# Diagonal products of two scan chunks in one run, for a one-core hybrid SSD and attention layer

## The chip, the cores and the metric

The kernel runs on one core of one Trainium2 chip. The metric is the device time of one execution in microseconds (us). The engines are named as in the profile: PE is TensorE (the matrix unit), PEld its weight loads, DVE is VectorE, ACT is ScalarE, POOL is GpSimd, SP is the engine that issues most DMA transfers. Every engine works through its own queue in order. They wait for one another through semaphores. PSUM is the memory that PE writes to, in banks of 128 partitions by 512 fp32 numbers.

## The reference

One layer of a diffusion backbone over 512 latent tokens of width 1024, with 256 context tokens beside them. A projection feeds two mixers, a bidirectional state-space scan (SSD) and windowed attention. Their outputs are gated, merged and projected, and a gated convolutional FFN follows. The part that matters here is the scan. It has 32 heads in four groups of eight; a head has 64 channels and the state 128 entries. The tokens are worked in chunks of 128, so four latent chunks per group:

```python
cb = jnp.einsum('bclgn,bcsgn->bgcls', cc, bc)
scores = cb[:, :, None] * jnp.exp(segsum(ac))
y_diag = jnp.einsum('bgrcls,bcsgrp->bclgrp', scores, xc)
y_off = jnp.einsum('bclgn,bcgrpn,bgrcl->bclgrp', cc, states[:, :-1], jnp.exp(cs))
```

`y_diag` is the **diagonal product**: a chunk's 128 by 128 matrix of scores and decays for each head, times the chunk's inputs. `y_off` is the far part, which comes from the states of earlier (and, for the backward scan, later) chunks. Afterwards a skip term `d_skip * xs` is added, and the sum is multiplied with the gate `silu(z)`; the row sums of its squares go into an RMS norm before the output projection of the branch. All of it is fp32.

## The kernel before, in words

Most of PE's work is large projections. Each fp32 operand is split into a high and a low part, and three matmuls replace one (`gemm`, lines 238, 239 and 241). The weights come by DMA and are split on the way: ACT casts the high part (line 183) and DVE subtracts it (line 184). The scan of group g is woven into the projections for group g+1, and in the last group into projections of the gates `z` and `g`. The scan's small steps are put between the steps of a `gemm` through the list `BETWEEN`, of which `gemm` takes one entry at every third step.

For one chunk c of a group the scan does this:

- `chunk_in(c)` loads the decays (`fb`), makes the score matrix `cb` on PE (line 1696), and takes its diagonal (`cbd`, line 1698) for the skip coefficient `coef`. For c > 0 POOL makes a diagonal matrix `dg` (line 1709) that carries the skip. ACT builds two tiles `E` of four heads each and, in two PSUM banks `eb`, the other direction's decays (lines 1719 and 1722). DVE merges them (line 1723), ACT takes the exponential (line 1726), and DVE multiplies with `cb` (line 1730). For c > 0 POOL adds `dg` (line 1732).
- `chunk_out(c)` is a **cluster** of fp32 matmuls on PE: the far products of both directions (line 1754, 16 passes), then the diagonal products of the eight heads into the bank `yd` (line 1762, 16 passes), then the new forward state (`advance`, line 1597, not for c = 3). The diagonal products have only 64 channels each, so PE works them in its 128 by 64 shape, two heads side by side. The other matmuls use the full 128 by 128 shape. DVE scales the far parts by the decays into `te` (line 1756), and POOL adds the two into `y` (line 1770).
- `late()` runs some steps of a projection later. For c = 0 only, where there is no `dg`, PE adds the skip to `yd` by transposing a tile `dx` into it (line 1778). DVE adds `yd` to `y` (line 1779). POOL multiplies with the gate into `zs` (line 1785), or DVE does for c = 3 (line 1783). Squares of the group before are summed by ACT and POOL (`square`, lines 1570 and 1571): in `late` of chunks 0 and 3 and in `chunk_in` of chunks 2 and 3, for all groups but the first.

After the fourth chunk `gate()` stores the four gated tiles of the group (`yz_d`, line 1798). After the last group the kernel loads these tiles back (line 1840), splits them (lines 1842 and 1843) and starts the branch's output projection.

The order on each engine is made by a planner that simulates the program and takes, on each engine, the ready instruction that stands earliest in the program. A few instructions are pinned behind the one before them on their engine (`keep_in_program_order`). POOL's operations of the scan are all pinned (`gp`, `gs`), so POOL goes through them strictly as they are written. PSUM banks called `mis` (five of them) serve `cb`, `eb`, the far products, `yd`, the state products and the transposes. The buffers in question: `E` has three buffers, `y` one (tag `tf`), the gate tiles two (tag `zs`), and the tag `th` one buffer that `dx` and the squares `sq` share.

Of the kernel before, what the change touches and what calls it, by code (L numbers as in the profile page):

```python
# [9 lines left out]
F32 = mybir.dt.float32  # L10
# [3 lines left out]
ALU = mybir.AluOpType  # L14
# [4 lines left out]
P = 128  # L19
# [25 lines left out]
def tile_hybrid_layer(  # L45
# [32 lines left out]
    V, S, G, T = nc.vector, nc.scalar, nc.gpsimd, nc.tensor  # L78
# [3 lines left out]
    hpool = ctx.enter_context(tc.tile_pool(name="hpool", bufs=1))  # L82
# [13 lines left out]
    def bank(name):  # L96
        pool, w = banks_[name]
        return pool.tile([P, 512 * w], F32, tag=name, name=name)
# [11 lines left out]
    def misb():  # L110
        return bank("mis")
# [3 lines left out]
    def tmp(tag):  # L115
        return tpool.tile([P, 512], F32, tag=tag, name=tag, bufs=TMP[tag])
# [27 lines left out]
    for j, t in enumerate((wdn[0], DSUMS[1], DSUMS[2], DSUMS[5], DSUMS[4], wdn[1], wdn[3])):  # L144
        for u in range(DU):
            n = min(2, DK - 2 * u) * HC
# [99 lines left out]
    ident = cpool.tile([P, P], F32, name="ident")  # L246
# [181 lines left out]
    with tc.tile_pool(name="spool", bufs=1) as sp:  # L428
# [237 lines left out]
        for j in range(KT):  # L666
# [46 lines left out]
            x = ("hi", "lo") if j >= NU else ("hh", "hl")  # L713
# [31 lines left out]
        for n in range(2):  # L745
            for j in range(KT):
                x = ("hi", "lo") if j >= NU else ("hh", "hl")
# [668 lines left out]
    zp = zpool.enter_context(tc.tile_pool(name="zpool", bufs=1, side="right", reuse_waits="tile"))  # L1416
    bp = bpool.enter_context(tc.tile_pool(name="bpool", bufs=1, reuse_waits="tile"))
# [15 lines left out]
    def flat(a):  # L1433
        return a.rearrange("p a b -> p (a b)")

    def h8(a):
        return a.rearrange("p (h d) -> p h d", h=8)

    def bc64(a):
        return a.unsqueeze(2).to_broadcast([P, 8, 64])  # L1440
# [132 lines left out]
    def gp(*a):  # L1573
        return tc.keep_in_program_order(G.tensor_tensor(*a))
# [4 lines left out]
    def ssd_steps(g):  # L1579
        d = GR[g]  # L1580
# [10 lines left out]
        def weigh_in(dr, c, place="xw"):  # L1591
            return weigh(d["xs"], c, TD[:, c, dr, 8 * g : 8 * g + 8], place)

        def advance(s, dr, c, xw):
            z0 = 32 * dr + 8 * g
            ps = misb()
            T.matmul(ps, d["Bk"][:, c, :], xw, start=True, stop=True)  # L1597
            n = new_state(dr)
            gp(h8(n), h8(s), bc64(eT[:, z0 : z0 + 8, c]), ALU.mult)
            V.tensor_tensor(n, n, ps, ALU.add)  # L1600
            return n
# [63 lines left out]
        def far_in(c, g=g):  # L1665

            far = bp.tile([P, 2, 4, P], F32, tag="far", name="far", bufs=2)
            for u in range(2):
                a = bass.AP(
                    tensor=us_d.tensor, offset=us_d[c, u, 0, g].offset, ap=[[0, 64], [16 * P, 2], [1, 512]]  # L1670
                )
                dma = nc.sync.dma_start(far[64 * u : 64 * u + 64].rearrange("p r j t -> p r (j t)"), a)
                if not g and not c:
                    tc.add_manual_dep(dma.ins, M_LOADS["x", 16].ins.name, QUEUED, reason="decays behind a projection's weights")
            GR[g]["far", c] = far

        def chunk_in(c):
# [4 lines left out]
            for dr in range(2):  # L1682
                f = bp.tile([P, 8, P], F32, tag="fb", name="fb", bufs=4)
                a = bass.AP(
                    tensor=cs_d.tensor, offset=cs_d.offset + (32 * dr + 8 * g) * L + c * P, ap=[[0, P], [L, 8], [1, P]]
                )
# [3 lines left out]
                fb.append(f)  # L1690
            d["E"] = []

# [18 lines left out]

            def decays():
                for q in range(2):
                    E = bp.tile([P, 4, P], F32, tag="E", name="E", bufs=3)
                    eb = misb()
                    F4 = fb[0][:, 4 * q : 4 * q + 4, :]
                    for u in range(4):
                        h = 8 * g + 4 * q + u
                        e0 = S.activation(E[:, u, :], F4[:, u, :], AF.Identity, bias=TX[:, c, 0, h : h + 1])
                        if u == 0 and c:  # L1720
                            tc.keep_in_program_order(e0)
                        S.activation(eb[:, u * P : (u + 1) * P], fb[1][:, 4 * q + u, :], AF.Identity, bias=TX[:, c, 1, h : h + 1])
                    V.copy_predicated(E, sel.unsqueeze(1).to_broadcast([P, 4, P]), eb.rearrange("p (h l) -> p h l", h=4))
                    d["E"].append(E)
                for E in d["E"]:
                    S.activation(flat(E), flat(E), AF.Exp)

# [18 lines left out]
        def chunk_out(c):  # L1746
            xs, E, far = d["xs"], d["E"], d.pop(("far", c))
            tok = slice(c * P, (c + 1) * P)
            parts = []
            for dr, s in ((0, d["Sf"]), (1, d["Sb"][c])):  # L1750
                ps = misb()
                for ct in range(4):
                    z = slice(ct * P, (ct + 1) * P)
                    T.matmul(ps[:, z], s[:, z], d["CT"][:, tok], start=True, stop=True)  # L1754
                t = tmp("te")
                V.tensor_tensor(t, ps, flat(far[:, dr]), ALU.mult)
                parts.append(t)

            yd = misb()
            for h in range(8):  # L1760
                o = yd[64 * (h % 2) : 64 * (h % 2) + 64, (h // 2) * P : (h // 2 + 1) * P]
                T.matmul(o, xs[:, c, h * 64 : (h + 1) * 64], E[h // 4][:, h % 4, :], start=h < 2, stop=c > 0 and h > 5)
            dx = None
            if not c:
                dx = zp.tile([P, 512], F32, tag="th", name="dx", bufs=1)
                gp(h8(dx), h8(xs[:, c, :]), bc64(d["coef"]), ALU.mult)
            if c < 3:
                d["Sf"] = advance(d["Sf"], 0, c, weigh_in(0, c))
            y = bp.tile([P, 512], F32, tag="tf", name="y", bufs=1)
            gp(y, parts[0], parts[1], ALU.add)  # L1770

            def late():

                if c < 3:
                    far_in(c + 1)
                for ct in range(0 if c else 4):
                    z = slice(ct * P, (ct + 1) * P)
                    tc.keep_in_program_order(T.matmul(yd[:, z], dx[:, z], ident, start=False, stop=ct == 3, is_transpose=True))
                tc.keep_in_program_order(V.tensor_tensor(y, yd, y, ALU.add))
                z = d["zt"][:, :, tok]  # L1780
                x = y.rearrange("p (a t) -> p a t", a=4)
                if c == 3:
                    V.tensor_tensor(z, x, z, ALU.mult)
                else:
                    gp(z, x, z, ALU.mult)
                if g and c in (0, 3):
                    square()

            assert not BETWEEN
            if g < 3:  # L1790
                BETWEEN.extend([lambda: None] * 4 + [lambda: (late(), turn(1)), turn])
            else:
                BETWEEN.extend([lambda: None] * 2 + [late])
# [116 lines left out]
    q2 = hpool.tile([P, L], F32, name="q2")  # L1910
# [535 lines left out]
```

## Time and profile before

| what | value |
|---|---|
| median of three runs | 1214.91 us (1214.61 to 1216.62) |
| the profiled execution | 1215.35 us, of which its span 1213.6 us |
| busy PE, DVE, ACT, POOL | 99%, 76%, 56%, 22% of the span |
| granted PE clock | 0.999 of full speed |
| the stretch with the scans | about 430 to 716 us |

The profile shows one execution. The span runs from the first to the last instruction, and 1.75 us of the profiled execution's time lie outside it. Busy PE says little by itself here, because overlapping matmuls count as busy; what counts is how far apart two neighbours start. In rows of the timeline the columns are start, duration, engine, line, operation, tiles and count, with idle time and its releaser in brackets. In rows of the chain of waits they are start, length, engine, tile, line and count.

### The profile page before, as it was taken

The page shows a single profiled execution, that of the slowest core. Times are in us where ns is not written, and L with a number is a line of the kernel's source. Part 1 is how long each engine was busy: PE and PEld are TensorE (multiplying, and loading weights), DVE is VectorE, ACT ScalarE, POOL GpSimd, SP SyncE. Part 2 cuts the span into 40 slices and gives each one's busy share as a digit, 9 for nine tenths or more (in the row PEclk, how much of TensorE's full clock was granted, in tenths as well). Part 3 has the DMA queues.
Part 4 walks back from the last instruction along what each step waited for, and adds up shares of the span by engine and source line. Part 5 has one row for each costly group of instructions (what it writes and reads, how often), then busy time and mean ns, then how long its engine had stood idle before and what let it go on. Part 6 is the DMA issues. An engine that isn't in the chain of part 4 may idle for free.

```text
span 1213.6 us, 17847 instructions
## 1 busy us (share of the span) xinstructions
PE 1203.6 (99%) x6429; PEld 1005.6 (83%) x6429; DVE 918.6 (76%) x1476; ACT 684.4 (56%) x1269; POOL 263.8 (22%) x274
## 2 busy tenths in 40 slices
PE   9999999999999999999999999999999999999998
PEld 6798888888878878788787887888988888888886
DVE  4857887888565588788887978677677767668787
ACT  4557887778543467476575664223544343436654
POOL 0000121100102546264382762000200100110021
PEclk9999999999999999999999999999999999999999
DMA  9655889844747737566477668687266634437662
GB/s 367 253 148 185 161 229 271 170 133 139 170 140 240 228 113 199 157 162 192 145 178 264 176 228 265 221 251 242 50 163 148 195 117 138 130 107 226 213 185 97
DMA packets 129417, 224.30 MB, mean 185 GB/s; under 512 B 27336, under 2 KB 70640, under 8 KB 129328
## 3 DMA queue, kind: packets, MB, share of 16 engines
q1 hardware_dynamic: 115248, 195.61, 52.0%
q0 software_dynamic: 13792, 27.27, 10.1%
q8 instruction: 51, 0.84, 0.3%
q14 instruction: 38, 0.31, 0.1%
q10 hardware_dynamic: 288, 0.27, 0.1%
HBM read 196.17 MB, written 45.02 MB: 199 GB/s over the span
## 4 chain that ended last, share of the span: by engine, by line
PE 90%; DMA 3%; DVE 2%; POOL 2%; issue 1%; ACT 1%; SPq 0%; DVEq 0%; POOLq 0%; ACTq 0%
PE acc L241 18%; PE acc L238 18%; PE acc L239 18%; PE score L979 3%; PE po L1028 3%; PE pt L1015 2%; PE mis L582 2%; PE mis L1754 2%; PE mis L1597 2%; PE mis L2304 2%; PE mis L2302 2%; PE mis L2303 2%; DMA xs_d<-xb 1%; PE acc L2304 1%; PE acc L2302 1%
## 5 line engine op out<-in xcount | busy, mean ns | idle before, releaser
L184 DVE TENSOR_TENSOR wlo<-wraw,whi 128x1024 fp32r<-128x1024 f32 (+1 forms) x115 | 148.3, 1289 | 89.2 <-ACT whi L183 88.3
L183 ACT CAST whi<-wraw 128x1024 fp32r<-128x1024 f32 (+1 forms) x115 | 120.2, 1046 | 154.2 <-PE acc L239 103.4
L238 PE MATMUL acc<-hlh,whi 128*128 128x512 f32 x472 | 192.8, 409 | 0.0
L241 PE MATMUL acc<-hlh,wlo 128*128 128x512 f32 x472 | 185.6, 393 | 0.0
L239 PE MATMUL acc<-hll,whi 128*128 128x512 f32 x472 | 185.0, 392 | 0.0
L238 PE MATMUL acc<-mh,whi 128*128 128x512 f32 x368 | 143.3, 389 | 0.0
L239 PE MATMUL acc<-ml,whi 128*128 128x512 f32 x368 | 143.2, 389 | 0.0
L241 PE MATMUL acc<-mh,wlo 128*128 128x512 f32 x368 | 143.2, 389 | 0.0
L241 PEld LDWEIGHTS acc<-hlh,wlo 128*128 128x128 f32 x472 | 88.6, 188 | 19.9 <-issue 0.5
L238 PEld LDWEIGHTS acc<-hlh,whi 128*128 128x128 f32 x472 | 88.8, 188 | 17.6 <-issue 2.8
L239 PEld LDWEIGHTS acc<-hll,whi 128*128 128x128 f32 x472 | 88.9, 188 | 17.4 <-issue 2.2
L238 PEld LDWEIGHTS acc<-mh,whi 128*128 128x128 f32 x368 | 69.1, 188 | 14.4
L241 PEld LDWEIGHTS acc<-mh,wlo 128*128 128x128 f32 x368 | 69.1, 188 | 14.3
L239 PEld LDWEIGHTS acc<-ml,whi 128*128 128x128 f32 x368 | 69.1, 188 | 14.2
L164 POOL DMA_DIRECT2D dsum<-wdn x24 | 25.3, 1118 | 194.3 <-DVE wlo L1112 183.7
L988 DVE CUSTOM_DVE_ANT_0 p<-score,winm,nsink 128x512 f32<-128x512 f32 (+1 forms) x64 | 51.8, 810 | 15.3 <-PE score L979 13.8
L995 ACT ACTIVATE p<-p,mneg 128x512 f32<-128x512 f32 (+1 forms) x64 | 49.7, 777 | 15.4 <-DVE mneg L988 14.9
L813 DVE SCALAR_TENSOR_TENSOR tm<-wraw,csil,tm 128x512 f32<-128x512 f32 x56 | 45.9, 819 | 13.1 <-DMA wraw<-wm 12.4
L1023 DVE TENSOR_TENSOR ptl<-pt,pth 128x512 fp32r<-128x512 f32 x72 | 47.5, 685 | 8.4 <-ACT pth L1019 7.7
L238 PE MATMUL acc<-hch,whi 128*128 128x256 f32 x176 | 53.2, 302 | 0.0
L1112 DVE TENSOR_TENSOR wlo<-wraw,whi 128x1024 fp32r<-128x1024 f32 x30 | 36.7, 1223 | 18.3 <-ACT whi L1109 18.2
L241 PE MATMUL acc<-hch,wlo 128*128 128x256 f32 x176 | 49.8, 283 | 0.0
(458 smaller groups left out, 3054.3 us busy)
## 6 DMA issues: line engine op xcount, KB each, us to landing
wraw<-wup SPq DMA_DIRECT2D x44, 512.0 KB, 4.0
dsum<-wdn POOLq DMA_DIRECT2D x24, 704.0 KB, 8.7
wraw<-wm SPq DMA_DIRECT2D x32, 512.0 KB, 4.1
fb<-cs_d SPq DMA_DIRECT2D x32, 512.0 KB, 7.5
wraw<-wx SPq DMA_DIRECT2D x24, 512.0 KB, 4.1
wm<-wm SPq DMA_DIRECT2D x16, 512.0 KB, 7.9
wraw<-wz SPq DMA_DIRECT2D x16, 512.0 KB, 4.7
far<-us_d SPq DMA_DIRECT2D x32, 256.0 KB, 5.1
```

Of the source, the lines that this page charges most:

```text
L183: F["cast"] = S.copy(hi[:, :n], r[:, :n])
L184: F["sub"] = V.tensor_tensor(lo[:, :n], r[:, :n], raw(hi[:, :n]), ALU.subtract)
L238: T.matmul(ps, wh, xh[:, k0 + k, :], start=a, stop=False)
L239: T.matmul(ps, wh, xl[:, k0 + k, :], start=False, stop=False)
L241: T.matmul(ps, wl, xh[:, k0 + k, :], start=False, stop=b)
L813: V.scalar_tensor_tensor(acc, r[:, u * 512 : u * 512 + 512], sc, acc, ALU.mult, ALU.add)
L988: V.tensor_tensor_reduce(p[:, :w], d["ps"][i][:, o0 : o0 + w], m, op0=ALU.add, op1=ALU.min, scale=1.0, scalar=nsink[:, h : h + 1], accum_o ...
L995: S.activation(p, p, AF.Exp, bias=d["mneg"][:, i : i + 1], scale=-1.0, accum_out=d["den"][:, i : i + 1])
L1023: V.tensor_tensor(d["ptl"][x], d["pt"][x], raw(d["pth"][x]), ALU.subtract)
L1112: sum_step(V.tensor_tensor(d["w"][1], d["r"], raw(d["w"][0]), ALU.subtract), 1 + (4 <= g < 12))
L2302: T.matmul(ps, h, wh, start=st, stop=False, skip_group_check=True)
L2304: T.matmul(ps, h, wl, start=False, stop=en, skip_group_check=True)
```

## The change

For chunks 0 and 2 the diagonal products are held back and done in the cluster of chunk 1 or 3, ahead of that chunk's own, so that sixteen heads' products stand in one run. In the last group only chunks 0 and 1 are treated so; chunks 2 and 3 stay as they were. `late` of the later chunk then finishes both chunks, with the transposes of `dx` for chunk 0 there. The tiles live longer, so some move: the second `E` of an odd chunk goes into a buffer with the tag `rbc4`, and the `y` of a held chunk into one with the tag `q2`, both idle at this time. The square that stood in `late` of chunk 0 moves to `late` of chunk 1. The skip term itself is computed as before.

```diff
             def decays():
                 for q in range(2):
-                    E = bp.tile([P, 4, P], F32, tag="E", name="E", bufs=3)
+                    if c % 2 and q:
+                        E = hpool.tile([P, 4, P], F32, tag="rbc4", name="E")
+                    else:
+                        E = bp.tile([P, 4, P], F32, tag="E", name="E", bufs=3)
...
-            yd = misb()
-            for h in range(8):
-                o = yd[64 * (h % 2) : 64 * (h % 2) + 64, (h // 2) * P : (h // 2 + 1) * P]
-                T.matmul(o, xs[:, c, h * 64 : (h + 1) * 64], E[h // 4][:, h % 4, :], start=h < 2, stop=c > 0 and h > 5)
-            dx = None
+            held = c == 0 or c == 2 and g < 3
+            d.setdefault("held", []).append((c, E))
+            done = []
+            for n, Es in [] if held else d.pop("held"):
+                yd = misb()
+                for h in range(8):
+                    o = yd[64 * (h % 2) : 64 * (h % 2) + 64, (h // 2) * P : (h // 2 + 1) * P]
+                    T.matmul(o, xs[:, n, h * 64 : (h + 1) * 64], Es[h // 4][:, h % 4, :], start=h < 2, stop=n > 0 and h > 5)
+                done.append((n, yd))
             if not c:
-                dx = zp.tile([P, 512], F32, tag="th", name="dx", bufs=1)
+                dx = d["dx"] = zp.tile([P, 512], F32, tag="th", name="dx", bufs=1)
                 gp(h8(dx), h8(xs[:, c, :]), bc64(d["coef"]), ALU.mult)
             if c < 3:
                 d["Sf"] = advance(d["Sf"], 0, c, weigh_in(0, c))
-            y = bp.tile([P, 512], F32, tag="tf", name="y", bufs=1)
+            y = hpool.tile([P, 512], F32, tag="q2", name="y") if held else bp.tile([P, 512], F32, tag="tf", name="y", bufs=1)
             gp(y, parts[0], parts[1], ALU.add)
+            d["y", c] = y
 
             def late():
                 if c < 3:
                     far_in(c + 1)
-                for ct in range(0 if c else 4):
-                    z = slice(ct * P, (ct + 1) * P)
-                    tc.keep_in_program_order(T.matmul(yd[:, z], dx[:, z], ident, start=False, stop=ct == 3, is_transpose=True))
-                tc.keep_in_program_order(V.tensor_tensor(y, yd, y, ALU.add))
-                z = d["zt"][:, :, tok]
-                x = y.rearrange("p (a t) -> p a t", a=4)
-                if c == 3:
-                    V.tensor_tensor(z, x, z, ALU.mult)
-                else:
-                    gp(z, x, z, ALU.mult)
-                if g and c in (0, 3):
+                for n, yd in done:
+                    y = d.pop(("y", n))
+                    for ct in range(0 if n else 4):
+                        z = slice(ct * P, (ct + 1) * P)
+                        tc.keep_in_program_order(T.matmul(yd[:, z], d["dx"][:, z], ident, start=False, stop=ct == 3, is_transpose=True))
+                    tc.keep_in_program_order(V.tensor_tensor(y, yd, y, ALU.add))
+                    z = d["zt"][:, :, n * P : (n + 1) * P]
+                    x = y.rearrange("p (a t) -> p a t", a=4)
+                    if n == 3:
+                        V.tensor_tensor(z, x, z, ALU.mult)
+                    else:
+                        gp(z, x, z, ALU.mult)
+                if g and c in (1, 3):
                     square()
```

## The prediction

> **What bounds the kernel now.** I read the page first, for its engines and its chain of waits.
>
> ```profile
> span 1213.6 us, 17847 instructions
> PE 1203.6 (99%) x6429; PEld 1005.6 (83%) x6429; DVE 918.6 (76%) x1476; ACT 684.4 (56%) x1269; POOL 263.8 (22%) x274
> PE 90%; DMA 3%; DVE 2%; POOL 2%; issue 1%; ACT 1%; SPq 0%; DVEq 0%; POOLq 0%; ACTq 0%
> ```
>
> PE sets the end over most of the span, but a tenth of the chain is elsewhere. Busy time by stretch shows where: the last group's scan (672 to 716) and the start of the branch's output projection (716 to 738). The columns are stretch, length, then busy time with count for PE, PEld, DVE, ACT and POOL, then clock, DMA share and GB/s.
>
> ```profile
> 599.00:672.00 73.00, 73.00 (x435) 59.90 (x435) 60.65 (x90) 47.52 (x114) 41.45 (x38) 1.00 0.70 207
> 672.00:716.00 44.00, 44.00 (x272) 36.42 (x272) 37.13 (x50) 30.55 (x71) 37.67 (x32) 1.00 0.57 168
> 716.00:738.00 22.00, 20.74 (x91) 16.60 (x90) 19.02 (x20) 15.36 (x23) 6.66 (x4) 1.00 0.91 303
> ```
>
> In the third group PE is busy all the time and POOL 57% of it. In the last group POOL is at 86%, and after it PE idles by 1.26 us. The chain of waits through these stretches, cut to its turns:
>
> ```profile
> 676.08 0.22 PE mis L1696 x2
> ...
> 681.78 0.45 PE mis L1778 x4
> 682.32 0.40 DVE y L1779
> 685.37 1.21 DVE mod L824
> 687.93 1.41 POOL y L1574
> 689.36 0.69 DVE y L1779
> 693.47 0.61 DVE E L1730
> ...
> ...
> 695.50 1.75 POOL E L1574
> 697.25 2.28 POOL ssq L1571
> 699.52 2.22 POOL zs L1574
> ...
> 714.80 1.06 DVE zs L1783
> 715.87 0.33 SPq L1798
> ...
> 719.68 4.06 DMA ld<-yz_d
> ...
> 735.48 1.14 DVE wlo L184
> 736.67 0.50 PE acc L241
> ```
>
> Up to 682 the chain is PE. Then it leaves PE at chunk 0's skip transposes, runs through DVE and POOL to the last gated tile, goes through SP's stores and the loads behind them in SP's queue, and reaches PE again at 736.67. So time saved on PE before 682 reaches the end only if this chain, which I call the **tail**, comes earlier too. Time saved on PE between 682 and 736 shows up as more idle time there.
>
> **What joining two runs saves on PE.** First the chain, then the timeline of PE, with a state product that follows no diagonal products beside a cluster that has them.
>
> ```profile
> 433.02 0.86 PE mis L1597 x2
> ...
> 453.74 1.79 PE mis L1754 x16
> 455.52 1.02 PE mis L1762 x16
> 456.55 1.06 PE mis L1597 x2
> ...
> 547.13 1.09 PE mis L1762 x16
> ```
>
> ```profile
> 455.72 0.82 PE L1762 MATMUL mis<-E,xs 128*64 128x128 f32 x12
> ```
>
> The 16 passes take 1.02 us from the end of the far products to their own end, and the state product behind them takes 1.06 instead of 0.86. Together a run costs 1.02 + 0.20 = 1.22 us. The second row shows the last twelve passes, six pairs, alone: taking the last pair's own 0.28 off 0.82 leaves 0.54 for five steps, 0.108 to 0.11 a pair. Eight pairs without any entry or exit would cost 0.87. A second run joined to the first should cost just that, so a **joined pair saves 1.22 - 0.87 = 0.35 us**. The changes of array shape are what is saved, and they come once per run. The price lies between 0 (the runs don't join) and 0.35 (nothing else is in a run that could shrink); I take 0.35, since the entry and exit are alike in all these rows.
>
> There are seven joins: chunks 0 and 1 in four groups, 2 and 3 in three. Six come before the last group: 6 x 0.35 = 2.1 us, and 0.07 for the one run that now lasts 1.09 and is chunk 2's, where I take the extra for a late `E`. So the last group starts **2.2 us earlier**. PE's total saving is 7 x 0.35 + 0.07 = 2.5 us.
>
> The other edits of the first three groups I cost at nothing. Their additions and gate products on POOL stay the same in number and lie in its idle 43%; without that cover each costs about 1.3 us, the length of a sum in the rows below. DVE's y addition of chunk 0 moves behind chunk 1's cluster with the same 0.69 us. The far loads stay where they were in SP's queue, and no DMA is added. The two moved buffers (`rbc4`, `q2`) take no instruction, and let ACT start on `E` before the diagonal products of the chunk ahead are read. The stores of a group's gated tiles now wait for chunk 2's gate product on POOL as well as for chunk 3's on DVE. Both follow one late step, so I allow 0 to 0.6 us there, half of that product, and take 0, as PE's weights for some steps are loaded by then.
>
> **What happens to the tail.** POOL works through its pinned operations in order. Before (start, length, operation):
>
> ```profile
> 683.09 1.27 POOL L1574 TENSOR_TENSOR zs<-y,zs 128x512 f32<-128x512 f32 x1
> 684.32 2.25 POOL L1571 TENSOR_TENSOR ssq<-ssq,sq 128x512 f32<-128x512 f32 x1
> 686.53 1.06 POOL L1574 TENSOR_TENSOR st<-st,eT 128x512 f32<-128x512 f32 x1
> 687.93 1.40 POOL L1574 TENSOR_TENSOR y<-te 128x512 f32<-128x512 f32 x1 [0.34 <-DVE te L1756]
> ...
> 694.24 3.01 POOL L1574 TENSOR_TENSOR E<-E,dg 128x512 f32<-128x512 f32 x2 [1.76 <-DVE E L1730]
> ...
> 712.74 1.30 POOL L1574 TENSOR_TENSOR y<-te 128x512 f32<-128x512 f32 x1
> ```
>
> From 694.24 to 714 POOL has no wait, so POOL sets the end of the tail from chunk 2's `E` on. The change takes the first two operations, gate product and square of chunk 0, from ahead of this point to behind it. They took 1.27 + 2.25 = 3.5 us there. The same sum of squares takes less where DVE leaves POOL alone, and DVE's work beside these two was long as well:
>
> ```profile
> 544.63 1.28 POOL L1571 TENSOR_TENSOR ssq<-ssq,sq 128x512 f32<-128x512 f32 x1
> 548.02 0.47 DVE L824 TENSOR_TENSOR mod<-mod,vec 128x4 f32<-128x4 f32 x1
> 549.99 1.21 DVE L184 TENSOR_TENSOR wlo<-wraw,whi 128x1024 fp32r<-128x1024 f32 x1
> 683.53 1.92 DVE L184 TENSOR_TENSOR wlo<-wraw,whi 128x1024 fp32r<-128x1024 f32 x1
> 685.37 1.22 DVE L824 TENSOR_TENSOR mod<-mod,vec 128x4 f32<-128x4 f32 x1
> ```
>
> The moved pair costs 2.6 us (1.28 each) to 4.5 (2.25 each); I take 3.0, nearer to the free price because the end of the tail already has POOL's stretched forms in it. **Plus 3.0.**
>
> The other way, chunk 2's `E` should be ready earlier, counted from the last group's start. Four things leave its way. PE reaches chunk 1's cluster 1.22 us earlier without chunk 0's run, and 0.45 more without the transposes: 1.7. The y addition of 682.32 goes from DVE: 0.7. The split and the small addition at 683.53 and 685.37 lose POOL as a neighbour: 0.71 + 0.75 = 1.4. The y addition of 689.36, which waited for POOL's y, moves behind the transposes: 0.7. Together 4.5. Against it stands PSUM: the joined run holds two of the five `mis` banks until `late`, and the next chunk's `cb` and two `eb` have to fit into the three left. I let the second `eb` wait for the state product's bank instead of a far product's, one DVE addition of 0.69 with its hand-over, 0.8. That leaves **minus 3.7**. The bounds are 5.5, where POOL's idle 1.76 goes as well, and -0.5, worked out under the slower rival.
>
> ACT's first square in chunk 2 shares a buffer with `dx`, so it and POOL's sum behind it now wait for the transposes in `late`. What queues behind that sum on POOL is the gate products, the next state and everything to the end. The transposes came 5.3 us after the cluster before (676.3 to 681.6); the same distance puts them at about 691.5, while POOL is with `E` until then at the earliest. I cost this wait at 0, up to 0.6.
>
> The sum: 3.0 - 3.7 - 2.2 = **-2.9 us** at the tail's end, and the idle time at 736.67 passes that on to the end one to one. The limit is PE itself: its own 2.5 plus the 1.26 us that it idles there now, -3.8. The profiled execution's 1215.35 (span 1213.6 and 1.75 around it) becomes 1212.4; it stands 0.44 over the median of 1214.91, so I predict **1212.0** for the median.
>
> [...]
>
> **Rivals.** (1) Slower. The second `eb` gets a bank of the joined run and so waits for the y addition behind the transposes, at about 692. Four ACT copies, the merge, the exponential and the product take then 1.3 + 0.7 + 0.6 + 0.7, and POOL's second `E` starts near 696.0 instead of 695.5: instead of 3.7 earlier, 0.5 later. With the pair at 4.5 the tail ends 4.5 + 0.5 - 2.2 = 2.8 us later, 1217.7. For it speaks that five banks are all taken within one cluster today. Against it speaks that the planner sees the banks. It decides from the point where POOL's `E` starts later, against the group's start, than it does now. 15%.
>
> (2) The tail keeps only part. DVE has other work to put into the gaps (weight splits and modulation sums), so `E` comes 1.5 us earlier instead of 3.7: 3.0 - 1.5 - 2.2 = -0.7, 1214.2. For it: the chain names DVE at five turns. Against it: POOL waits 1.76 us there today. 27%.
>
> (3) The change doesn't do what it says. The planner finds chunk 0's products ready early and PE with a gap, and places them apart from chunk 1's. No shape change is saved, and the 2.2 is gone: `E` keeps 3.7 less the 1.22 of the earlier cluster: 3.0 - 2.5 = +0.5, 1215.4. Against it: all sixteen runs stand whole in the clusters now. 10%.
>
> **How the numbers follow.** The forecast has 48%, with its own range from -3.8 to -2.0, 1211.1 to 1212.9. No change means within 0.2%, 2.4 us, about what a measurement of this kernel can tell. Of the forecast I put 0.40 beyond that and 0.08 within; rival (2) gives 0.02 and 0.25, rival (3) 0.09 within and 0.01 slower, rival (1) 0.13 slower and 0.02 within. That makes 0.42 faster, 0.44 the same, 0.14 slower. The range goes from 1210.8, the limit of PE less the 0.3 us by which the fastest run shown lies under the median, to 1217.0, which leaves out half of rival (1) and little else.
>
> **What would show it.** Nine runs of line 1762 instead of sixteen, seven of them of 32 passes and near 1.02 + 0.87 = 1.9 us; the state products in the clusters of chunks 0 and 2 (but the last group's chunk 2) at 0.86. The last group's far products of chunk 0 about 2.2 us earlier than 672.06. POOL's `E` of chunk 2 at about 688 instead of 694.24, and the stores that stand at 715.87 at about 713. The idle time of PE before 736.67 at 1.26 + 2.5 - 2.9 = 0.9 us. I am wrong if the stores come later than 715.87, if a new wait for a `mis` bank stands in ACT's or PE's rows, or if PE waits for `E` in a joined run.

## The result, and the profile after

The changed kernel takes **1229.16 us** (median of four, 1227.2 to 1229.31), against 1215.38 for the kernel before on the same chip (1214.61 to 1216.62): a ratio of 1.0108, 95% interval 1.0096 to 1.012. It is 1.1% slower, where 1212.0 was predicted. The profiled execution took 1229.09 us.

The page of the changed kernel, engines and shares of the chain of waits:

```profile
span 1227.3 us, 17825 instructions
PE 1206.3 (98%) x6429; PEld 1007.6 (82%) x6429; DVE 916.9 (75%) x1476; ACT 683.9 (56%) x1269; POOL 262.6 (21%) x274
PE 82%; DVE 6%; ACT 3%; DMA 3%; issue 3%; POOL 2%; SPq 0%; POOLq 0%; DVEq 0%; ACTq 0%
```

The span grew by 13.7 us, and PE's share of the chain fell from 90% to 82%: the time went into waits of PE. Two landmarks divide it: the first far products of group 0 (440.47 before, 440.49 now) and those of the last group (672.06 and 678.99). The **scans** of the first three groups between them took 231.6 us before and take 238.5: 6.9 more. The **rest**, from there to the end, takes 6.8 more (541.5 and 548.3).

The joined run itself came out as predicted. Timeline of PE, the cluster of chunk 1 in the first group and, below it, PE's waits in the scans:

```profile
451.93 1.95 PE L1757 MATMUL mis<-CT,st 128*128 128x128 f32 x16
453.81 1.97 PE L1769 MATMUL mis<-E,xs 128*64 128x128 f32 x32
...
457.38 0.49 PE L1696 MATMUL mis<-CT,BT 128*128 128x128 f32 x2 [0.55 <-DVE te L1759]
...
469.65 1.16 PE L1757 MATMUL mis<-CT,st 128*128 128x128 f32 x8 [1.44 <-ACT xs L1549]
...
549.05 2.02 PE L1757 MATMUL mis<-CT,st 128*128 128x128 f32 x16 [2.03 <-ACT xs L1549]
...
579.78 0.44 PE L1450 MATMUL mis<-ident,tc 128*128 128x128 f32 x2 [0.69 <-DVE tc L1431]
...
629.50 1.16 PE L1757 MATMUL mis<-CT,st 128*128 128x128 f32 x8 [1.04 <-ACT xs L1549]
```

The 32 passes stand together. Line numbers moved: far products 1757, diagonal products 1769, y addition 1789, merge 1726. The rows below the joined run are of a new kind: PE waits, three times at chunk 2's far products (469.65, 549.05 and 629.50). In the kernel before PE never waits in the scans. The list of PE's waits from 440 to 679 (engine, tile, line, releaser; total, times, longest; for the kernel before this list is empty from 440 to 672):

```profile
PE mis L1757 <- ACT xs L1549: 4.5, 3, 2.0
PE mis L1450 <- DVE tc L1431: 2.3, 3, 1.3
PE mis L1696 <- DVE te L1759: 0.5, 1, 0.5
```

That is 7.3 us. Measured as the distance between neighbours, which also takes in that a far product behind a wait took up to 0.377 us (the median is 0.275), they are 8.5; less 2.1 for six joins leaves 6.4 of the 6.9.

The last group in the chain of waits (start, length, engine, tile, line):

```profile
690.72 9.37 DMA wraw<-wm
700.18 0.76 DVE tm L813
700.97 0.75 DVE tm L813
701.72 0.66 DVE E L1726
...
706.40 2.26 POOL ssq L1571
708.67 2.52 POOL zs L1574 x2
711.18 2.25 POOL ssq L1571
...
718.31 3.48 POOL E L1574 x2
721.84 1.12 PE mis L1769 x8
722.97 0.72 PE acc L238
723.69 0.43 PE acc L239
...
728.35 0.23 PE acc L238
```

And the same place in the timeline of DVE, POOL, PE and SP:

```profile
700.18 1.54 DVE L813 SCALAR_TENSOR_TENSOR tm<-wraw,csil,tm 128x512 f32<-128x512 f32 x2 [4.90 <-DMA wraw<-wm]
701.64 1.35 DVE L1726 COPY_PREDICATED E<-sel,mis 128x512 f32<-128x512 uint8 x2
...
703.93 2.53 POOL L1574 TENSOR_TENSOR E<-E,dg 128x512 f32<-128x512 f32 x2 [5.84 <-DVE E L1733]
...
719.63 0.66 PE L1769 MATMUL mis<-E,xs 128*64 128x128 f32 x8 [2.27 <-POOL E L1574]
721.84 1.12 PE L1769 MATMUL mis<-E,xs 128*64 128x128 f32 x8 [1.55 <-POOL E L1574]
...
727.43 2.03 SPq L1808 DMA_DIRECT2D yz_d<-zs  x4
```

DVE stands 4.90 us at line 813, a sum over a modulation matrix, until its weights land. Behind it in DVE's queue is the merge of chunk 2's decays, which has nothing to do with these weights. In the kernel before, the merge got through first:

```profile
689.97 1.60 DVE L813 SCALAR_TENSOR_TENSOR tm<-wraw,csil,tm 128x512 f32<-128x512 f32 x1
691.49 1.35 DVE L1723 COPY_PREDICATED E<-sel,mis 128x512 f32<-128x512 uint8 x2
692.74 0.73 DVE L813 SCALAR_TENSOR_TENSOR tm<-wraw,csil,tm 128x512 f32<-128x512 f32 x1
```

The sum at 689.97 still belongs to the weight tile before. The first sum over the tile in question stands at 692.74, behind the merge, and finds its weights landed.

So POOL starts chunk 2's `E` at 703.93 instead of 694.24, and PE waits for chunk 3's `E`. Twelve matmuls then follow at steps of 0.43 us instead of 0.23, while the granted PE clock is 0.50. By stretch (columns as before):

```profile
606.00:679.00 73.00, 70.33 (x425) 57.87 (x424) 57.94 (x86) 45.55 (x111) 39.91 (x38) 1.00 0.69 204
679.00:723.00 44.00, 38.91 (x246) 31.67 (x244) 32.95 (x47) 25.41 (x61) 32.78 (x30) 0.98 0.54 159
723.00:745.00 22.00, 22.00 (x87) 17.98 (x88) 15.80 (x17) 14.76 (x24) 9.66 (x8) 0.88 0.76 247
```

PE loses 5.1 us in the last group's stretch, where it lost nothing before, and in the third stretch its granted clock is 0.88.

### The profile page after: what moved, and what is told of

The parts are those of the page before. It is cut to its first block, busy times and chain, and to the rows that moved or that the text cites. A ratio compares the mean times of both kernels' runs of the same rounds, so it can differ in the third digit from the quotient of the medians.

```text
span 1227.3 us, 17825 instructions
## 1 busy us (share of the span) xinstructions
PE 1206.3 (98%) x6429; PEld 1007.6 (82%) x6429; DVE 916.9 (75%) x1476; ACT 683.9 (56%) x1269; POOL 262.6 (21%) x274
## 4 chain that ended last, share of the span: by engine, by line
PE 82%; DVE 6%; ACT 3%; DMA 3%; issue 3%; POOL 2%; SPq 0%; POOLq 0%; DVEq 0%; ACTq 0%
PE acc L241 17%; PE acc L238 16%; PE acc L239 16%; PE score L979 3%; PE po L1028 3%; PE pt L1015 2%; PE mis L582 2%; DMA xs_d<-xb 2%; PE mis L1757 1%; PE mis L2313 1%; PE mis L2312 1%; PE mis L2314 1%; PE acc L2313 1%; PE acc L2312 1%; PE acc L2314 1%
## 5 line engine op out<-in xcount | busy, mean ns | idle before, releaser
L988 DVE CUSTOM_DVE_ANT_0 p<-score,winm,nsink 128x512 f32<-128x512 f32 (+1 forms) x64 | 51.9, 811 | 15.4 <-PE score L979 13.9
L995 ACT ACTIVATE p<-p,mneg 128x512 f32<-128x512 f32 (+1 forms) x64 | 49.7, 777 | 15.4 <-DVE mneg L988 14.8
```

Of the source, the lines that this page charges most:

```text
L988: V.tensor_tensor_reduce(p[:, :w], d["ps"][i][:, o0 : o0 + w], m, op0=ALU.add, op1=ALU.min, scale=1.0, scalar=nsink[:, h : h + 1], accum_o ...
L995: S.activation(p, p, AF.Exp, bias=d["mneg"][:, i : i + 1], scale=-1.0, accum_out=d["den"][:, i : i + 1])
```

## The experiments

**First theory**: the loss of the first three groups is a shortage of `mis` banks, because two stay taken from the joined run until the later chunk is finished. **Its rival**: the first three groups lose nothing by themselves, and everything hangs on the tail. **For the last group**: DVE standing at the load, against the moved POOL pair. Scans and rest are each compared with those of the kernel before (231.6 and 541.5 us), from one profile of each kernel.

| kernel | median us | ratio (95%) | scans | rest |
|---|---|---|---|---|
| changed kernel | 1229.16 | 1.0108 (1.0096 to 1.0120) | +6.9 | +6.8 |
| joins in the last group only | 1220.45 | 1.0043 (1.0028 to 1.0058) | +0.1 | +4.9 |
| joins in the first three only | 1220.94 | 1.0051 (1.0037 to 1.0066) | +5.9 | -0.4 |
| changed, six `mis` banks | 1239.30 | 1.0198 (1.0182 to 1.0213) | +2.2 | +19.3 |
| before, six `mis` banks | 1232.45 | 1.0150 (1.0133 to 1.0167) | -0.2 | +15.4 |
| before, four `mis` banks | 1223.08 | 1.0066 (1.0051 to 1.0082) | +5.1 | +3.5 |
| first three, finished early | 1218.58 | 1.0030 (1.0019 to 1.0040) | +1.4 | -0.1 |
| all four, finished early | 1223.86 | 1.0074 (1.0059 to 1.0089) | +2.5 | +4.7 |
| chunks 0 and 1 only, first three | 1220.76 | 1.0047 (1.0032 to 1.0062) | +5.5 | +0.4 |
| last group only, sums behind the merge | 1216.41 | 1.0012 (1.0003 to 1.0022) | +1.1 | +1.7 |
| changed, sums behind the merge | 1224.49 | 1.0077 (1.0064 to 1.0091) | +6.8 | +1.3 |
| chunks 2 and 3 only, early | 1219.84 | 1.0038 (1.0026 to 1.0051) | +4.7 | 0.0 |
| chunks 2 and 3 only, late | 1222.24 | 1.0058 (1.0046 to 1.0071) | +7.6 | 0.0 |
| before, `E` buffer moved, no join | 1220.06 | 1.0042 (1.0027 to 1.0058) | +4.8 | -0.2 |
| chunks 2 and 3 only, early, ACT's order kept | 1214.75 | 0.9998 (0.9989 to 1.0006) | -0.6 | -0.3 |
| first three, early, ACT's order kept | 1217.25 | 1.0019 (1.0010 to 1.0028) | +1.5 | +0.1 |

The time ahead of the scans is in neither column. Each column comes from one profile, and a difference of about 1 us between two scans proves little by itself. In "last group only, sums behind the merge" the first three groups are written as before, and still PE waits 0.95 us at 639.11, which makes most of the 1.1.

### Which groups lose

The joins in the last group only; the other kernel has the same with `g < 3` in all three places, and for chunks 2 and 3 too:

```diff
-                    if c % 2 and q:
+                    if q and (c == 1 and (g == 3) or c == 3 and (False)):
-            held = c == 0 or c == 2 and g < 3
+            held = c == 0 and (g == 3) or c == 2 and (False)
-                if g and c in (1, 3):
+                if g and c in (1 if g == 3 else 0, 3):
```

> Joins chunks 0 and 1 in the last group only; the first three groups are as before. Theory (two separate losses, both from the two PSUM banks that a joined run holds until late): the last group's own share of the changed kernel's loss, from 6.9 us at its start to 13.7 at the end, appears alone: about +6.8 us, 1222. Rival (the last group lost only because it came 6.9 us late against its weight loads): between -1 and +2 us, 1214 to 1217, with no long wait of DVE at line 813.

> Joins in groups 0 to 2 only; the last group is as before. Theory (two separate losses): the last group starts 6.9 us late as in the changed kernel and passes that on, +5.5 to +6.9 us, 1221 to 1222. Rival (the loss before the last group is hidden by the idle time behind it): at most +5.6, 1220.5; rival (all the loss comes from the last group): -2 us, 1213.

Measured: 1220.45 and 1220.94, so +5.2 and +5.7. Both parts lose, and in different places: the first only behind the start of the last group, the second only before it. Together they make 10.9 of 13.8 us. In the whole change the scans lose 1.0 more than alone (6.9 against 5.9) and the rest 1.9 more (6.8 against 4.9). Part of the latter is PE's granted clock: it is 0.50 for 6.83 us behind the waits of the last group in the changed kernel, and for 3.41 us in the kernel with joins in the last group only. The rival, that all hangs on the tail, falls.

### Banks

The changed kernel with six `mis` banks instead of five, and the kernel before with the same; the sixth is taken from the accumulators:

```diff
-    psum_pools(mis=(5, 1), acc=(3, 1))
+    psum_pools(mis=(6, 1), acc=(2, 1))
```

> The changed kernel with six mis banks and two acc banks in place of five and three. Theory (PE waits for banks that the joined run holds): against the control with the same banks and no joins, faster by 1 to 3 us, and the waits of PE at lines 1696 and 1757 in the joined clusters are gone. Rival (DVE and POOL get two chunks' finishing work at once and come late with the convolutions): against the control still slower by 6 us or more.

> Control: the kernel before with six mis banks and two acc banks. Either theory: not faster than 1214, as no wait for a mis bank costs time before; slower, up to 1225, if the projections need their third acc bank.

Measured: 1239.3 and 1232.45. By the total the expectation missed: the changed kernel stays 6.9 us over its partner, as the rival had it. Two accumulators instead of three cost 15.4 us behind the scans without any join, and 19.3 with the joins; there PE waits 3.9 us for `E` in the last group, as in the changed kernel. That part is the last group's, which is taken up below. The scans can be compared: the changed kernel is 2.4 us over its partner there (233.8 and 231.4), against 6.9 with five banks. PE's waits of the changed kernel with six banks, 440 to 672:

```profile
PE mis L1450 <- DVE tc L1431: 1.9, 2, 1.2
PE acc L238 <- DVE ta L1424: 1.0, 1, 1.0
PE mis L1757 <- ACT xs L1549: 0.5, 1, 0.5
```

The waits in chunk 2's far products shrink from 4.5 to 0.5 us: these were the banks. The waits of the transposes at line 1450 for DVE remain: these are not.

The counter-test takes a bank away where nothing is joined:

```diff
-    psum_pools(mis=(5, 1), acc=(3, 1))
+    psum_pools(mis=(4, 1), acc=(3, 1))
```

> The kernel before, with no joined run, but with four mis banks instead of five (the acc banks stay three). Theory (one bank less through a cluster and its late steps is enough to make PE wait): PE waits at line 1696 or 1757 in the clusters, and the time is 4 us or more longer, 1219 or more. Rival (the joined run's loss comes from something else that the join moves): within 1 us of 1215.4.

Measured: 1223.08, +7.8 us, of which 5.1 in the scans. One bank fewer, without any join, costs 5.1 us there, where the joins cost 6.9. For the 3.5 us in the rest the trace shows three things: PE waits 2.0 us for DVE's split of weights and 0.7 for `E`, and its granted clock is 0.50 for 3.41 us from 740.69.

Where the bank is held can be read in the timeline of the changed kernel at 469 us:

```profile
469.03 0.57 ACT L1549 COPY xs<-mis 128x512 f32<-128x512 f32 x1
...
469.77 1.28 DVE L1789 TENSOR_TENSOR y<-mis,y 128x512 f32<-128x512 f32 x2
```

By the profile, PE resumed at 469.65 in a bank that ACT's copy had just read. The two banks of the joined run, made from 453.81 to 455.78, come free only with the two y additions at 469.77, 14 us later.

### Finishing the earlier chunk at once

If the held banks are the cause, the earlier chunk should be finished (transposes, y addition, gate product) right behind the joined run instead of one late step further. In the first three groups, and in a second kernel in all four:

```diff
+            if len(done) == 2:
+                finish(*done.pop(0))
+
             def late():
                 if c < 3:
                     far_in(c + 1)
                 for n, yd in done:
-                    y = d.pop(("y", n))
...
+                    finish(n, yd)
```

> Joins in groups 0 to 2 only, and the earlier chunk of a joined run is finished (its skip transposes, its addition to y, its gate product) right behind the run, so that its bank is free again within some 2 us instead of at late. Theory (the joined run's second bank is what PE waits for): the waits of PE at lines 1696 and 1757 shrink from 5.7 us to under 1, and the time falls from 1220.9 to between 1213 and 1216. Rival (DVE has two chunks' additions on top of the convolutions): 1219 to 1222, as the additions stay.

> As the run with early finishing, but with the join in the last group too, as in the changed kernel. Theory (the last group's loss of about 5 us is a wait of its own): 1218 to 1221. Rival (the last group suffers from the held bank alone): 1213 to 1216.

Measured: 1218.58 and 1223.86. Both lie over what I had expected, 1213 to 1216 and 1218 to 1221. In the scans the loss of the first three groups falls from 5.9 to 1.4 us, so 4.6 of it goes with early finishing. The waits in the far products, 4.5 us, are gone, which fits the held banks; but the edit also moves DVE's additions, and the waits at line 1450 fall with it, from 1.6 to 0.4 us. In the second kernel the rest still loses 4.7 us, so the last group's loss is not the held bank. PE's waits in the scans of the first of these kernels (440 to 679):

```profile
PE mis L1696 <- ACT xsc L1549: 0.9, 1, 0.9
PE mis L1597 <- ACT xsc L1549: 0.5, 1, 0.5
PE mis L1450 <- DVE tc L1431: 0.4, 1, 0.4
```

They are shorter, but not gone. Measured between neighbours they are 2.3 us and eat up the 2.1 that six joins save; some 1.1 us of the 1.4 I find in no row. In the profile 1.7 us are lost ahead of group 0's scan, where the kernels don't differ in their work; another execution of this kernel may not show that.

### The pairs one by one

Chunks 0 and 1 only, in the first three groups (`held = c == 0 and (g < 3) or c == 2 and (False)`, and the two other conditions to match):

> Joins of chunks 0 and 1 alone, in groups 0 to 2. Theory (the bank waits sit in the cluster of chunk 2, behind a joined chunk 1): 5.7 us of waits less 3 x 0.35 saved, +4.6, 1219.9. Rival (waits come from chunk 3's joined run and the next group's start just as much): +2 us or less, 1217.

Measured: 1220.76, +5.3 us where both pairs together cost 5.7; the scans of its profile lose 5.5 against 5.9. PE's four waits all lie between chunk 1's run and the end of chunk 2's far products, as expected. But the profile is of the slowest of four executions, and PE's granted clock is 0.50 in it for 3.41 us from 551.28. Chunk 3's far products behind that come 1.5 us late without any wait. Without this the pair costs about 4.0 in the scans, so it is not shown that nearly the whole loss lies in this pair. I took it so: then chunks 2 and 3 should by themselves be nearly free. Only they, finished early and finished late:

```diff
-            held = c == 0 or c == 2 and g < 3
+            held = c == 0 and (False) or c == 2 and (g < 3)
```

> Joins of chunks 2 and 3 alone, in groups 0 to 2, with the earlier chunk finished right behind the run. No state product and no score matrix follow in that cluster, so four banks do. Theory (banks, and DVE's heap of work in late): no wait of PE at lines 1696 and 1757, and 3 x 0.35 = 1.05 us gained less at most 0.5 of waits at line 1450, 1214.4 to 1215.0. Rival (every join brings its own wait): 1216.5 or more.

> Joins of chunks 2 and 3 alone, in groups 0 to 2, finished in late as in the changed kernel. Theory (here the loss is DVE's: two additions and a gate product at once, ahead of the convolution that the transposes of line 1450 wait for): waits of PE at line 1450 of 1.5 to 2.5 us, the time 0.5 to 1.5 us over the kernel before, 1216 to 1217. Rival (only the banks count): 1214.4, as in the run with early finishing.

Measured: 1219.84 and 1222.24, losses of 4.5 and 6.9 us, where no bank was short by my theory. Both expectations missed. (Some 1.7 us of the second kernel's scans is again a granted clock of 0.50, from 459.59 for 3.41 us.) In these traces ACT stands for a load before the evictions of B, 2.5 to 3.9 us in each of the three groups, and PE waits for those evictions. The activations at which ACT stands belong to chunk 3's second `E`, the one that the change moved to the buffer `rbc4`. In the ring of three buffers it had to wait until chunk 2's products were read. In a buffer of its own nothing holds it back in the planner's simulation, and it gets ahead of the evictions. In the full change chunk 1's tile holds that buffer until chunk 1's run, and no such wait appears.

This theory against "a join of chunks 2 and 3 costs by itself" was put to two kernels. The kernel before, with the buffer moved and nothing joined:

```diff
-                    E = bp.tile([P, 4, P], F32, tag="E", name="E", bufs=3)
+                    if q and c == 3 and g < 3:
+                        E = hpool.tile([P, 4, P], F32, tag="rbc4", name="E")
+                    else:
+                        E = bp.tile([P, 4, P], F32, tag="E", name="E", bufs=3)
```

> The kernel before, with one edit: in the first three groups chunk 3's second decay tile lies in the other buffer, as in the change. Nothing is joined, nothing moved behind anything. Theory (the buffer alone moves the decays ahead in ScalarE's order, and ScalarE then stands for their load): five waits of TensorE of about 1 us each as in the run with chunks 2 and 3 joined, without the 1.05 us that the joins saved: 1220 to 1221.5 us. Rival (the join costs, the buffer is innocent): 1215.3, no new wait.

Measured: 1220.06, +5.2 us for a buffer that takes no instruction. Its timeline of ACT:

```profile
451.64 0.39 ACT L1722 ACTIVATE E<-fb,TX 128x128 f32<-128x128 f32 x1
455.82 0.69 ACT L1722 ACTIVATE E<-fb,TX 128x128 f32<-128x128 f32 x2 [3.79 <-DMA fb<-cs_d]
456.42 0.35 ACT L1516 COPY Bkc<-mis 128x256 f32<-128x256 f32 x1
456.67 0.63 ACT L1430 ACTIVATE tb<-ta 128x512 f32<-128x512 f32 x1
```

ACT stands 3.79 us for `fb` of chunk 3, whose load was issued at 449.18 and landed at 455.72. The eviction `Bkc` behind it, whose transposes on PE had ended at 451.97, comes at 456.42. In the kernel before it came at 452.70:

```profile
452.35 0.39 ACT L1719 ACTIVATE E<-fb,TX 128x128 f32<-128x128 f32 x1
452.70 0.38 ACT L1516 COPY Bkc<-mis 128x256 f32<-128x256 f32 x1
454.11 0.63 ACT L1430 ACTIVATE tb<-ta 128x512 f32<-128x512 f32 x1 [1.03 <-DVE ta L1424]
```

The other kernel keeps the join and the buffer, and ties that `E` to its old place in ACT's order:

```diff
+                        if q and c == 3 and g < 3:
+                            tc.add_manual_dep(e0.ins, F["exp"].ins.name, QUEUED, reason="behind the decays before")
...
-                    S.activation(flat(E), flat(E), AF.Exp)
+                    F["exp"] = S.activation(flat(E), flat(E), AF.Exp)
```

> The run with only chunks 2 and 3 joined (first three groups, the earlier chunk finished right behind the run) with one thing more: chunk 3's second decay tile, which lies in the buffer of its own, may be begun on ScalarE only behind chunk 2's exponentials. ScalarE's order around the context half of B is then that of the kernel before. Theory (ScalarE stood 3.7, 3.5 and 2.5 us at chunk 3's decays, which the new buffer let the planner put ahead of the evictions of B, and TensorE waited for those evictions): the five waits of 0.9 to 1.6 us in the clusters of chunks 1 and 2 go, three joins save 0.35 us each, 1214.4 us (1213.8 to 1215.5), against 1219.8 without the order. Rival (a join of chunks 2 and 3 costs by itself, by its banks or the later adds): 1218 to 1220, with the waits in the same places.

Measured: 1214.75, ratio 0.9998: 5.1 us better than without the tie (4.7 with each run set against its own kernel before), and level with the kernel before. The theory holds in both directions. The scans are 0.6 us shorter, 1.05 from three joins less one wait of 0.44 us behind 546.92. Group by group it is clearer: after the first and the third join, where nothing waits, the next group's far products come 0.32 and 0.34 us earlier. That is the join's price, seen alone.

The same tie in the kernel with both pairs, finished early (`q and c % 2 and g < 3`):

> Both pairs joined in the first three groups, the earlier chunk finished right behind the run, and the second decay tile of chunks 1 and 3 begun on ScalarE only behind the exponentials of the chunk before it. Theory: where chunk 1's tile holds that buffer, chunk 3's can't run ahead, so the order is worth little here: the banks decide as before, 1217.5 to 1219 against 1218.6 without the order. Rival (ScalarE standing at a load is the larger part of what the joins cost in the first three groups here too): 1213.5 to 1215.5.

Measured: 1217.25, just under the range of the theory; scans +1.5 against +1.4 without the tie. In the scans the order is worth nothing here, as the theory said. The medians differ by 1.3 us (0.8 with each run set against its own kernel before). This may come from ahead of the scans, where the profile of the kernel without the tie lost 1.7; no run settles that.

### DVE behind a load

In the kernel with joins in the last group only, three sums over two weight tiles (all at line 813) are tied behind the merge of that group's chunk 2. PE's and ACT's orders stay the same:

```diff
-                    V.scalar_tensor_tensor(acc, r[:, u * 512 : u * 512 + 512], sc, acc, ALU.mult, ALU.add)
+                    x = V.scalar_tensor_tensor(acc, r[:, u * 512 : u * 512 + 512], sc, acc, ALU.mult, ALU.add); i in (8, 9) and tc.add_manual_dep(x.ins, F["merged", 3, 2].ins.name, QUEUED, reason="behind the decays")
...
-                    V.copy_predicated(E, sel.unsqueeze(1).to_broadcast([P, 4, P]), eb.rearrange("p (h l) -> p h l", h=4))
+                    F["merged", g, c] = V.copy_predicated(E, sel.unsqueeze(1).to_broadcast([P, 4, P]), eb.rearrange("p (h l) -> p h l", h=4))
```

> Join in the last group only, and two modulation steps of DVE (line 813) are kept behind the merge of chunk 2's decays in DVE's order; nothing else differs on PE and ACT. Theory (DVE stands 4.5 us before a weight load of 9.5 us, with the merge queued behind it): the 4.5 us go, 1215 to 1216.5 instead of 1220.5. Rival (the merge is late because its eb tiles wait for banks): at most 1 us goes, 1219.5 or more.

The same sums tied in the whole change:

> The changed kernel with the two modulation steps kept behind the merge of chunk 2's decays in the last group; nothing else differs on PE and ACT. Theory (the last group's loss is DVE before a weight load): 4 to 5 us less than the changed kernel, 1224 to 1225. Rival (with the late start the load lands in time): no difference, 1228 to 1229.

Measured: 1216.41 instead of 1220.45, and 1224.49 instead of 1229.16: 4.0 and 4.7 us gone. DVE and POOL in the second of them:

```profile
695.57 0.74 DVE L1726 COPY_PREDICATED E<-sel,mis 128x512 f32<-128x512 uint8 x1 [1.04 <-ACT mis L1725]
696.74 0.75 DVE L1726 COPY_PREDICATED E<-sel,mis 128x512 f32<-128x512 uint8 x1 [0.43 <-ACT mis L1725]
...
699.52 0.90 DVE L813 SCALAR_TENSOR_TENSOR tm<-wraw,csil,tm 128x512 f32<-128x512 f32 x1 [0.21 <-DMA wraw<-wm]
...
698.22 3.35 POOL L1574 TENSOR_TENSOR E<-E,dg 128x512 f32<-128x512 f32 x2 [0.89 <-PE acc L239]
```

The merge comes 6 us earlier, and the wait for the weights falls from 4.90 to 0.21. PE's waits for `E` fall from 3.8 us to 1.4, and the granted clock no longer falls behind them, which had cost another 2.4. What is left of the last group's loss, 1.3 us, I put down to the POOL pair and the waits for `E`; that was not tested by itself.

## Why the prediction was wrong, point by point

**0.35 us per join: right.** The timeline has the 32 passes in 1.97 us, and the interval from chunk 0's far products to chunk 1's in the first group fell from 13.10 to 11.44, by the 1.22 and 0.45 worked out. The state product of chunk 0 there, which now stands behind far products, takes 0.87 (442.27 to 443.14), where the one behind diagonal products took 1.06 (456.55 before). With ACT's order kept, the two joins of chunks 2 and 3 behind which nothing waits brought the next group forward by 0.32 and 0.34.

**"The last group starts 2.2 us earlier": wrong, and this is the larger half.** It starts 6.9 later. The failing step is "The other edits of the first three groups I cost at nothing". That sentence looked at POOL, DVE and SP, and not at PSUM, which I costed for the last group alone, though the joined run holds two of five banks in all of them. The code to see it was there: `cb`, two `eb`, two far products, `yd`, the state product and the transposes all share these five banks within one chunk. A bank fewer costs 5.1 us in the scans (measured without a join), finishing early gives back 4.6 us (with less waiting at line 1450 in it), and a sixth bank takes 4.5 us out. About 2.3 us of waits at line 1450 come from DVE and not from banks; they stay with six banks (1.9) and shrink to 0.4 when the earlier chunk is finished at once. Some 0.5 us of the 6.9 I can't assign to a row.

**"The two moved buffers ... let ACT start on E before": the words were right and the sign wrong.** I counted the earlier start as a freedom. By itself the moved buffer costs 5.2 us, since ACT takes an `E` whose load is still under way ahead of the eviction and stands for it (3.79 us at 455.82). In the scans of the whole change ACT never waits for that load; I put this down to chunk 1's tile, which occupies the buffer there.

**`E` of chunk 2 earlier by 3.7: wrong.** Counted from the group's start, POOL begins it 24.9 us later (703.93 - 678.99) instead of 22.2: 2.8 later. The four things I took out of its way went (the cluster of chunk 1 alone comes 1.65 us earlier, for 1.7), but DVE, freed of them, came earlier to the sum at line 813 and stood 4.90 us for its weights. With the sums tied it is 19.3 (698.22 - 678.88): 2.8 earlier. So the mechanism was right up to a size of 2.8 for 3.7, and the failing step is that I treated DVE's gaps as free time and did not ask which instruction with a load stood next in its queue. Rival (2), "DVE has other work to put into the gaps", named the work, and took it for work without waits.

**The POOL pair, plus 3.0: right in size.** From chunk 2's `E` to the end of its last sum POOL takes 21.1 us before (694.24 to 715.30) and 24.4 with the sums tied (698.22 to 722.66), 3.4 more; in the changed kernel itself it is 1.9 more (there chunk 0's and chunk 1's gate products took 2.56 us together, and 4.03 with the sums tied). The sums of squares in the chain above took 2.26 and 2.25 us, both beside a split on DVE (line 184, at 705.98 and 710.31); the one at 632.87, with no row of DVE beside it, took 1.30. The 1.28 us at 544.63, from which the free price was taken, have DVE beside them for 0.52 us.

**Rival (1)**, a wait for a bank of the joined run, came true in another place: not at the second `eb` of the last group, but in chunk 2's far products of the groups before. In the kernel with the sums tied, the merge waits 1.04 and 0.43 us for ACT, so the tail of that rival is small.

**The signs I set.** Those of the joined run came true. The stores stand at 727.43 instead of 713 and new waits for `mis` banks appear, both on the wrong side. PE does wait 2.27 and 1.55 us for `E`, though in chunk 3's own run of the last group and not in a joined run.

The whole: 6.9 us in the first three groups, and 6.8 in the rest. Of the latter the tied sums take out 5.5 by the profiles (4.7 of the whole time by the medians), which is DVE at the load with what follows from it. The 1.3 left in the rest I put down to POOL's longer tail and the waits for `E`, which was not tested by itself.

By the rows of the changed kernel, the rest is 5.1 us of PE's waits in the last group and 2.4 of half clock behind them, less the 1.3 that PE idled at 736.67 before and 0.35 for the last join: 5.9 of the 6.8. A lost clock stood in no term of the prediction.

## What to carry to other kernels

A saving on the bounding engine is only as good as the resource that it holds longer: count the PSUM banks that are taken at each point of every repetition of the loop, not only at the end of the span (one bank fewer cost 5.1 us in the scans here). In a program that a planner orders, an instruction that becomes ready earlier, by a free buffer or a freed engine, can get in front of others in its engine's queue and stand there for a load (3.79 us on ACT and 4.90 on DVE here); ask of each such instruction which transfer it needs and who is behind it. A tie in the order gave back 4 to 5 us in three of the four kernels that had one.

## What the runs showed of the hardware that was not expected

Behind waits of 1.27 to 2.27 us PE's granted clock fell to 0.50 in the two kernels that follow. In the changed kernel PE idles 1.27, 2.27 and 1.55 us ahead of 715.22, 719.63 and 721.84, with short runs between. From 721.37 its granted clock is 0.50 for 6.83 us, and twelve steps take 0.43 us instead of 0.23: 2.4 us lost beside the waits. In the kernel with joins in the last group only and the sums tied, one wait of 1.55 us stands ahead of it, at 711.78: the clock is 0.50 from 712.84 for 3.41 us, with seven such steps from 713.01 on. The kernel before had a wait of 1.26 ahead of 736.67 without any, and the changed kernel one of 2.03 ahead of 549.05 without any, so the length of a wait alone doesn't decide.

The stretches of half clock that begin behind waits of the scans and the last group all last 3.41 or 6.83 us. In the 3.41 us ahead of the two falls above PE was still busy for 0.66 and 1.82 us. What decides over a fall no run here shows.

The load of one weight tile took 9.4 us from issue to landing (690.72 to 700.09) where a load of the same kind took 5.7 before, issued at 685.47. In four other kernels with the last group joined it took 8.8 to 9.5. Why is open.
